# A four-stage decoder step on one core: seven products over two token chunks, in three groups per stage

## The chip, the core and the metric

The kernel runs on one core of one Trainium2 chip. The metric is the device time of one execution, in microseconds; for a kernel the median of several executions is given. The profile is that of one execution, taken by the hardware profiler. Its engines are PE (TensorE: matmuls, and PEld, its weight loads), DVE (VectorE), ACT (ScalarE), POOL (GpSimd) and SP (SyncE, which here only issues transfers). PE, DVE and ACT carry out their instructions in the order of the source (`in_order` ties each to the one before it); the order of SP's and POOL's instructions is left to the scheduler of the program.

## The reference

One inference step of a small decoder, all in float32: 1024 prompt tokens and 8 decode tokens, width 2048. The tokens are cut into two chunks: chunk 0 has 512 prompt tokens, chunk 1 has the other 512 and the 8 decode tokens (520). There are four large stages, each a product of the activations (tokens x 2048) with a weight matrix:

```python
z = x @ w_in                                   # ai: 2048 -> 2 x 2048 (u and gate)
d, state = multiscale_pool(u, prefix, pos)     # trailing windows 2, 4, 8, 16 on four channel groups
y = (group_linear(d) * scale * silu(gate)) @ w_out          # ao: 2048 -> 2048
h = layer_norm(ALPHA * x + y)
k, v = rope(h @ w_k), h @ w_v                  # bi, with the next line: 2048 -> 512 + 2 x 2048
q, gate = rope(h @ w_q), h @ w_gate
o = attention(q, k, v, window=128, sinks)      # 32 heads of 64, 4 key heads
y = (o * silu(gate)) @ w_out                   # bo: 2048 -> 2048
out = layer_norm(ALPHA * h + y)
```

So ai has 32 output tiles of 128 channels, ao 16, bi 36 and bo 16. In each stage the contraction runs over 16 blocks of 128 channels.

## The kernel before

**A product in three matmuls.** Each float32 operand is split into a high and a low part (`float32r`): ACT casts the high part (L423 for weights, L686 for activations), DVE subtracts it to get the low part (L438, L695). A block product is then high x high + high x low + low x high, three matmuls that add up in one PSUM bank (L586 to L588). A weight entry is 128 x 1024, eight blocks of 128 x 128.

**Seven products instead of eight.** The stages work by the scheme of Strassen and Winograd: two output tiles, the even and the odd contraction blocks, and the two halves of one token chunk (256 or 260 columns) form a 2 x 2 block product, done with seven half-size products, numbered 0 to 6, instead of eight. The price is sums of weight blocks (DVE, L254 and L307, stored to memory by POOL and loaded again for chunk 1) and sums of activations (`t_ops`, L741 to L744, stored as tx, tg, th and to). `seven` (L510) runs the seven products of a pair of output tiles; each is 24 matmuls. The sums that the scheme needs of results are made as banks are emptied: L527 seeds a bank with a negated result, L533 and L536 save results, L542 and L559 copy out, L547 and L552 subtract.

**Which stages run how.** `PHASES` (L50) lists the work: ai, ao, bi and bo, each for chunk 0 and then for chunk 1. Two of the nine phases, named in `PLAIN` (L57), do not use seven products: channel group 0 of ai on chunk 0, and all of bi on chunk 0. There `unit` (L600) makes one output tile with 48 matmuls of 512 columns (L614 to L616).

**Order.** All of PE's work is written out in sequence; between products `end` (L460) lets in what is due: events at a step (`at`, `product`), a step of a side task (layer norm, sums of activations or weights), and loads and splits of the next phase's activations (`x_tick`). Weights are loaded, cast and split some entries ahead (`ahead`, L185). All of these live in 53 slots of SBUF, each 128 x 1040 float32, handed out by `Mem`. The last phase ends with three tile pairs in an order of their own (`TAIL`, L68), the last half of the layer norm, and its stores.

Of the kernel before, what the change touches and what calls it, by code (L numbers as in the profile page):

```python
# [16 lines left out]
P = 128  # L17
# [20 lines left out]

NP7 = 7


# [3 lines left out]
K_ID, K_MP, K_J, K_RC = 0, 128, 256, 384  # L47
N_CST = 384 + 4 * NST
# [5 lines left out]
PHASE_OF = {"x": "ai", "g": "ao", "h": "bi", "o": "bo"}  # L54
INPUT_OF = {k: x for x, k in PHASE_OF.items()}

PLAIN = (PHASES[0], PHASES[5])  # L57
STRASSEN = [(k, c) for k, c, part in PHASES if (k, c, part) not in PLAIN]
ORDER7 = (0, 2, 1, 5, 3, 4, 6)

LOCKED = (("ao", 0), ("ao", 1), ("bi", 1), ("bo", 0), ("bo", 1))
ORDERL = (0, 5, 2, 1, 3, 4, 6)
ENGINES = (mybir.EngineType.PE, mybir.EngineType.DVE, mybir.EngineType.Activation)
NSLOT = 53
KEEP0 = 1

SPLIT = 5, 6, 7
TAIL = (  # L68
    (5, 0), (5, 2), (5, 1), (6, 0), (5, 3), (5, 4), (6, 2), (6, 1), (7, 0), (6, 3), (7, 2), (7, 1), (6, 4),
    (7, 3), (7, 4), (5, 5), (5, 6), (6, 5), (6, 6), (7, 5), (7, 6),  # L70
)
X_KEEP = 5
X_AGE = 3
SIDE_KEEP = 5

DEC_AT = (0, 1, 6, 6, 7, 8, 9, 10, 13, 13), (11, 11, 12, 12, 13, 14, 15, 16, 17, 17)
# [76 lines left out]
class Entry:  # L153


    def __init__(self, loads, make, src, after):
        self.loads, self.make, self.src, self.after = loads, make, src, after


class Kern:  # L160
    def __init__(self, ctx, tc, io):
# [19 lines left out]
        self.n = 0  # L181
        self.i = self.e = self.lastO = self.turns = self.ring = 0
        self.posts, self.events, self.side = [], {}, []
        self.fresh = False
        self.ahead = 7, 4, 3  # L185
        dr = lambda n, s: dram.tile(s, F32, tag=n, name=n)
        self.Td, self.act, self.l_sq, self.l_sh = {}, {}, {}, {}
        for c, (_, T) in enumerate(CHUNKS):
            for n, k in (("x", "ai"), ("g", "ao"), ("h", "bi"), ("o", "bo")):
                if (k, c) in STRASSEN:  # L190
                    self.Td[n, c] = dr(f"t{n}{c}", [P, 8, 4, T // 2])
            self.act["x", c] = io[f"x{c}"]
            for n in ("g", "h", "o", "p"):
                self.act[n, c] = dr(f"{n}{c}", [P, NK, T])
        self.ws = {
            n: [dr(f"s{n}{q}", [P, 4, 1024]) for q in range(np_)]
            for n, np_ in (("wia", 16), ("woa", 8), ("wkv", 2), ("wib", 16), ("wob", 8))
        }
# [10 lines left out]
    def use_four(self, wide):  # L209

        if self.four is not None:
            self.four.__exit__(None, None, None)
            self.four = None
        self.wide = wide
        if wide is None:
            return
        self.four = self.tc.tile_pool(name=self.nm("ps4"), bufs=1, space=bass.MemoryType.PSUM)
        self.pool4 = self.four.__enter__()
        if not wide:
            self.S = self.pool4.tile([P, 2, 1024], F32, name=self.nm("pS"))  # L220

    def psW(self):
        if not self.wide:
            return self.psD()
        self.turns = (self.turns + 1) % 4
        return self.pool4.tile([P, 512], F32, tag=f"W{self.turns}", name=self.nm("pD"))
# [8 lines left out]
    def split(self, hi, lo, src):  # L235
        self.nc.scalar.copy(hi, src)
        self.nc.vector.tensor_sub(lo, src, hi.bitcast(F32))


    def quads(self, name, q):  # L240
        w = self.io[name]
        u, v = w[2 * q], w[2 * q + 1]
        return u[:, :1024], u[:, 1024:], v[:, :1024], v[:, 1024:]

    def load1(self, s, k, src):
        def go():
            s[k] = self.mem.full()
            self.nc.sync.dma_start(s[k].a[:, :1024], src)

        return go  # L250

    def add1(self, s, out, a, b, dst, *free):
        def go():
            self.nc.vector.tensor_add(s[out].a[:, :1024], s[a].a[:, :1024], s[b].a[:, :1024])  # L254
            self.nc.gpsimd.dma_start(dst, s[out].a[:, :1024])
            for k in free:
                s.pop(k).free(True)

        return go

    def plain_pair(self, name, q):

        a11, a12, a21, a22 = self.quads(name, q)
        ws = self.ws[name][q]
        s = {}
        ent = lambda k, src, after: Entry([self.load1(s, k, src)], [], lambda: s[k], after)
        late = [
            self.add1(s, "c", "b", "c", ws[:, 1, :]),
            self.add1(s, "b", "a", "b", ws[:, 0, :], "b"),
            self.add1(s, "a", "a", "c", ws[:, 2, :], "c"),  # L270
            self.add1(s, "d", "a", "d", ws[:, 3, :], "a", "d"),
        ]
        return [
            ent("a", a11, []),
            ent("d", a12, []),
            ent("b", a21, []),
            ent("c", a22, [lambda: self.late.extend(late)]),
        ]

    def lone(self, src):  # L280
        s = {}
        return Entry([self.load1(s, "a", src)], [], lambda: s["a"], [lambda: s.pop("a").free()])

    def next_pair(self, name, q):
        a11, a12, _, a22 = self.quads(name, q)
        w = self.ws[name][q]
        blk = {0: a11, 1: w[:, 2, :], 2: w[:, 1, :], 3: w[:, 0, :], 4: w[:, 3, :], 5: a12, 6: a22}
        ent = {i: self.lone(blk[i]) for i in ORDER7}
        for i in (1, 2, 3, 4):
            ent[i].loads.insert(0, lambda: self.sums(name, q))  # L290
        return ent

    def first_pair(self, name, q):

        a11, a12, a21, a22 = self.quads(name, q)
        ws = self.ws[name][q]
        s = {}

        def load(k, src):
            return self.load1(s, k, src)  # L300

        def add(out, x, y, i):
            def go():
                assert self.prepped >= self.made - 2
                if out not in s:
                    s[out] = self.mem.full()
                self.nc.vector.tensor_add(s[out].a[:, :1024], s[x].a[:, :1024], s[y].a[:, :1024])  # L307
                self.nc.gpsimd.dma_start(ws[:, i, :], s[out].a[:, :1024])
# [3 lines left out]
        def free(*ks):  # L312
            return [lambda k=k: s.pop(k).free(k != "c") for k in ks]

        ent = lambda k, loads, make, after: Entry(loads, make, lambda: s[k], after)
        return {
            0: ent("a", [load("a", a11)], [], []),
            2: ent("e", [load("b", a21), load("c", a22)], [add("e", "b", "c", 1)], []),
            1: ent("a", [], [add("b", "a", "b", 0), add("a", "a", "e", 2)], free("e")),
            5: ent("d", [load("d", a12)], [], []),  # L320
            3: ent("b", [], [], free("b")),
            4: ent("d", [], [add("d", "d", "a", 3)], free("a", "d")),
# [1688 lines left out]
```

## Time and profile before

| | |
|---|---|
| median of 3 executions | 2387.29 us (2386.95 to 2390.01) |
| profiled execution, first to last instruction | 2385.9 us (its span; the profile gives no other time of it) |
| TensorE busy | 2341.5 us, 98% |
| VectorE busy | 1877.5 us, 79% |
| ScalarE busy | 1304.0 us, 55% |
| moved by DMA | 653.25 MB, 274 GB/s over the span |
| granted TensorE clock | 0.997 |

The busy times are sums over an engine's instructions with overlaps taken out. Matmuls are pipelined, so TensorE's busy time tells whether it had work, not how fast it ran; how fast is read from how many matmuls of one shape start in a stretch of time. A row of a group of instructions has the line, engine, operation, the tiles written and read with their shapes, the count, then busy time and mean duration in ns, then the idle time just before these instructions and what ended it. A row of a transfer has the size and the median time from issue to landing.

### The profile page before, as it was taken

What the parts mean: (1) busy time and instruction counts of PE and PEld (TensorE: products, weight loads), DVE (VectorE), ACT (ScalarE), POOL (GpSimd) and SP (SyncE); (2) the same over time, 40 slices, a digit from 0 to 9 for tenths busy, and PEclk for the clock granted to TensorE, in tenths of its full rate; (3) what the DMA queues carried; (4) which work ended last, traced back from release to release, by engine and by line L of the source; (5) the groups of instructions that cost most, each with busy time, mean ns of one, the idle gap of its engine ahead of it and who ended that gap; (6) DMA issues with size and microseconds to landing.
All of it is one profiled execution on the core that took longest, in us unless ns stands there. A gap on an engine that the chain in (4) does not pass through costs nothing. (4 is left out here: it accounts for less than half of the span.)

```text
span 2385.9 us, 45076 instructions
## 1 busy us (share of the span) xinstructions
PE 2341.5 (98%) x17823; PEld 2198.3 (92%) x17823; DVE 1877.5 (79%) x2315; ACT 1304.0 (55%) x2363; POOL 211.3 (9%) x373
## 2 busy tenths in 40 slices
PE   8999999999999999999999999999999999999996
PEld 6899999999999999998778888899999999999996
DVE  8797999786788768868787777777776668788877
ACT  4454446444446446653564444575666668546654
POOL 0111110000000000000011111100000000000003
PEclk9999999999999999999999999999999999999998
DMA  8667779898889888987597777589776558699883
GB/s 292 242 222 275 252 262 381 305 314 293 298 305 350 310 275 312 363 287 279 188 330 268 255 276 247 194 284 306 251 243 204 172 179 296 223 345 365 296 278 135
DMA packets 250564, 653.25 MB, mean 274 GB/s; under 512 B 25457, under 2 KB 109169, under 8 KB 250353
## 3 DMA queue, kind: packets, MB, share of 16 engines
q1 hardware_dynamic: 206032, 489.50, 61.3%
q0 software_dynamic: 44320, 160.88, 17.5%
q8 instruction: 139, 2.28, 0.4%
q14 instruction: 73, 0.59, 0.1%
HBM read 459.41 MB, written 181.36 MB: 269 GB/s over the span
## 5 line engine op out<-in xcount | busy, mean ns | idle before, releaser
L586 PE MATMUL pD<-m,m 128*128 128x260 f32 (+1 forms) x4304 | 1220.7, 284 | 6.0 <-DVE m L547 2.9
L588 PE MATMUL pD<-m,m 128*128 128x260 f32 (+1 forms) x4304 | 1212.8, 282 | 4.1 <-DVE m L438 4.1
L587 PE MATMUL pD<-m,m 128*128 128x260 f32 (+1 forms) x4304 | 1213.4, 282 | 0.0
L438 DVE TENSOR_TENSOR m<-m,m 128x1024 fp32r<-128x1024 f32 x650 | 787.5, 1222 | 102.3 <-ACT m L423 67.6
L586 PEld LDWEIGHTS pD<-m,m 128*128 128x128 f32 x4304 | 810.4, 188 | 15.3 <-issue 7.4
L588 PEld LDWEIGHTS pD<-m,m 128*128 128x128 f32 x4304 | 810.9, 188 | 5.5 <-DVE m L438 5.3
L587 PEld LDWEIGHTS pD<-m,m 128*128 128x128 f32 x4304 | 810.4, 188 | 1.6 <-issue 1.4
L423 ACT CAST m<-m 128x1024 fp32r<-128x1024 f32 x650 | 675.9, 1048 | 238.8 <-DVE m L307 56.7
L614 PE MATMUL pD<-m,m 128*128 128x512 f32 x704 | 281.4, 400 | 8.0 <-ACT m L686 8.0
L615 PE MATMUL pD<-m,m 128*128 128x512 f32 x704 | 278.1, 395 | 0.5 <-DVE m L695 0.5
L616 PE MATMUL pD<-m,m 128*128 128x512 f32 x704 | 278.0, 395 | 0.0
L614 PEld LDWEIGHTS pD<-m,m 128*128 128x128 f32 x704 | 132.9, 189 | 42.4 <-ACT m L686 8.0
L615 PEld LDWEIGHTS pD<-m,m 128*128 128x128 f32 x704 | 133.0, 189 | 30.6 <-DVE m L695 1.0
L616 PEld LDWEIGHTS pD<-m,m 128*128 128x128 f32 x704 | 132.8, 189 | 30.7
L695 DVE TENSOR_TENSOR m<-m,m 128x1024 fp32r<-128x1024 f32 (+1 forms) x114 | 139.4, 1226 | 10.6 <-ACT m L686 4.7
L559 ACT COPY m<-pD 128x260 f32<-128x260 f32 (+1 forms) x75 | 28.1, 374 | 188.7 <-PE pD L588 188.4
L686 ACT CAST m<-m 128x1024 fp32r<-128x1024 f32 (+1 forms) x114 | 119.5, 1053 | 17.6 <-PE pD L616 6.2
L254 DVE TENSOR_TENSOR m<-m,m 128x1024 f32<-128x1024 f32 x88 | 107.6, 1222 | 1.9
L1499 ACT ACTIVATE m<-m,sm 128x128 f32<-128x128 f32 x256 | 99.3, 391 | 0.0
L547 DVE TENSOR_TENSOR m<-pD,m 128x260 f32<-128x260 f32 (+1 forms) x78 | 33.1, 424 | 81.4 <-PE pD L588 81.3
L954 PE MATMUL pD<-m,m 128*128 128x260 f32 (+1 forms) x528 | 91.3, 323 | 0.0
L552 DVE TENSOR_TENSOR m<-pD,m 128x260 f32<-128x260 f32 (+1 forms) x76 | 32.2, 424 | 70.7 <-PE pD L588 70.6
(199 smaller groups left out, 2153.3 us busy)
## 6 DMA issues: line engine op xcount, KB each, us to landing
m<-in_wia SPq DMA_DIRECT2D x112, 512.0 KB, 6.9
m<-in_wib SPq DMA_DIRECT2D x112, 512.0 KB, 5.1
swia<-m POOLq DMA_DIRECT2D x64, 512.0 KB, 4.7
m<-swia SPq DMA_DIRECT2D x64, 512.0 KB, 6.6
m<-swoa SPq DMA_DIRECT2D x64, 512.0 KB, 6.8
swib<-m POOLq DMA_DIRECT2D x64, 512.0 KB, 5.0
m<-swib SPq DMA_DIRECT2D x64, 512.0 KB, 5.3
m<-swob SPq DMA_DIRECT2D x64, 512.0 KB, 6.5
```

Source lines behind the costliest of these rows:

```text
L254: self.nc.vector.tensor_add(s[out].a[:, :1024], s[a].a[:, :1024], s[b].a[:, :1024])
L423: self.nc.scalar.copy(hi.r[:, :1024], self.stream[self.cast].src().a[:, :1024])
L438: self.nc.vector.tensor_sub(lo.r[:, :1024], s.src().a[:, :1024], hi.a[:, :1024])
L586: nc.tensor.matmul(ps[:, :TH], wh[:, s], h, start=new and k == 0, stop=False, skip_group_check=on)
L587: nc.tensor.matmul(ps[:, :TH], wh[:, s], l, start=False, stop=False, skip_group_check=on)
L588: nc.tensor.matmul(ps[:, :TH], wl[:, s], h, start=False, stop=k == 7, skip_group_check=on)
L614: nc.tensor.matmul(ps[:], wh[:, s], h, start=par == 0 and k == 0, stop=False)
L615: nc.tensor.matmul(ps[:], wh[:, s], l, start=False, stop=False)
L616: nc.tensor.matmul(ps[:], wl[:, s], h, start=False, stop=par == 1 and k == 7)
L686: self.nc.scalar.copy(h.r[:, :n], s.a[:, :n])
L695: self.nc.vector.tensor_sub(l.r[:, :n], s.a[:, :n], h.a[:, :n])
L1499: nc.scalar.activation(x["s3"][:, i, :], x["s3"][:, i, :], AF.Exp, bias=nm[:, i : i + 1], scale=0.125, accum_out=rs[:, i : i + 1],)
```

## The change

The kernel's schedule is written anew. All four stages now use seven products for every pair of output tiles, and the 2 x 2 blocks are cut differently: the two columns of blocks are the two token chunks themselves (512 and 520 columns) and no longer the two halves of one chunk. There is then one phase per stage and no plain one. A pair is two output tiles half a stage apart (`positions`); there are 50 pairs: 16 in ai, 8 in ao, 18 in bi, 8 in bo.

A weight entry, once split, serves 512 or 520 columns: products 0 and 5 as 24 matmuls of 512, the other five as 2 x 24 of 260. So there are 350 weight entries of pairs plus 16 of the group products, where before every chunk had its own.

Each stage runs in three groups, one after the other over all its pairs: A (products 0 and 5, which need only chunk 0 and give chunk 0's first tile), C (1, 3 and 6, which give chunk 0's second tile), and B (2 and 4, which give chunk 1's two tiles). What one group leaves for a later one goes through memory: product 0, negated, is stored after A and loaded to seed the banks of C (`seed`), and products 1 and 3 are saved as a pair after C and loaded in B (`recall`). The sums of weight blocks are made in C and two of them stored for B.

The layer norm of chunk 0 runs during group B, that of chunk 1 during group A of the next stage; attention of chunk 0 runs during A and C of bi, that of chunk 1 during B and the start of bo. Work beside the products is placed in two ways: at a fixed step (`on`, a step being 24 matmuls of 260 or 12 of 512 columns), or softly (`soft`), between an earliest step and a due step, when an estimate of DVE's and ACT's load (`meter`, `calm`) allows it.

```diff
-PHASES = (
-    ("ai", 0, (0, 1)), ("ai", 0, (1, 4)), ("ai", 1, (0, 4)), ("ao", 0, None), ("ao", 1, None), ("bi", 0, None),
-    ("bi", 1, None), ("bo", 0, None), ("bo", 1, None),
-)
...
-PLAIN = (PHASES[0], PHASES[5])
...
-ORDER7 = (0, 2, 1, 5, 3, 4, 6)
...
+GROUPS = (("A", (0, 5)), ("C", (1, 3, 6)), ("B", (2, 4)))
+JS = {"ai": (0, 1, 2, 3), "ao": (0, 1, 2, 3), "bi": (0, 1, 2, 3), "bo": (0, 2, 1, 3)}
...
+HV = slice(0, THM), slice(THM, TMAX)
+FULL = slice(0, TP)
...
+L_LOAD, L_CAST, L_LOW = 11, 6, 4
+SLACK = 1.5
+X_LOAD, X_CAST, X_LOW, X_FAR, X_SPARE = 9, 4, 3, 22, 8
...
+    def gentle(self):
+
+        self.meter()
+        while True:
+            best = None
+            for z in self.tasks:
+                if z[2] <= self.i and (best is None or z[:2] < best[:2]) and (z[0] <= self.i or self.calm(z[3])):
+                    best = z
...
+    def sums(self, t, ph, p):
...
+        for n, k, src in ((15, "b", a21), (14, "c", a22), (13, "a", a11), (12, "d", a12)):
+            self.on(t - n, load(k, src), 6)
+        def chain(n):
+            (add("e", "b", "c", ws[:, 0, :]), s3, add("a", "a", "e"), s4)[n]()
+            if n < 3:
+                self.soft("v", self.i, t - 8 + n, lambda: chain(n + 1))
+
+        self.soft("v", t - 11, t - 9, lambda: chain(0))
...
+    def run_unit(self, u):
...
+        wh, wl = (s.r for s in self.w_get(u))
+        last = self.lastu[ph, idx] is u
+        hs = u.hs[:1] if u.grp == "A" else u.hs
+        for n, cs in enumerate(hs):
+            w = cs.stop - cs.start
+            key = ph, pos, cs.start
+            if idx in (0, 2):
+                self.bank[key] = self.psD()
+            new = idx in (0, 2)
+            ps = self.bank[key]
+            for n2 in range(8):
+                j, kk = JS[ph][n2 // 2], n2 % 2
+                k = 2 * j + kk
+                hx, lx = self.x_get((ph, idx, j))
+                h, l = (a.rv(2, TMAX)[:, kk, cs] for a in (hx, lx))
+                s = slice(k * P, (k + 1) * P)
+                on = not new
+                nc.tensor.matmul(ps[:, :w], wh[:, s], h, start=new and n2 == 0, stop=False, skip_group_check=on)
+                nc.tensor.matmul(ps[:, :w], wh[:, s], l, start=False, stop=False, skip_group_check=on)
+                nc.tensor.matmul(ps[:, :w], wl[:, s], h, start=False, stop=n2 == 7, skip_group_check=on)
...
+    def post(self, u, cs):
...
+        if idx == 0:
+            s = self.mem.half()
+            nc.gpsimd.memset(s.a[:, w:], 0.0)
+            nc.scalar.mul(s.a[:, :w], ps[:, :w], -1.0)
+            nc.gpsimd.dma_start(self.n0[ph][:, pos, :], s.a)
+            s.free(True)
+        elif idx in (1, 3):
...
+            if ph in RES:
+                nc.vector.scalar_tensor_tensor(
+                    z, z, ALPHA, ps[:, :w], op0=ALU.mult, op1=ALU.add if i else ALU.subtract
+                )
+            else:
+                nc.scalar.copy(z, ps[:, :w])
+            if idx == 3 and fin:
+                nc.gpsimd.dma_start(self.bb[ph][:, pos], s.v(2, TMAX))
...
+        elif idx in (5, 6):
...
+            self.evac(ph, pos)(self.dest(ph, pos, m, 0)(cs), ps[:, : cs.stop - cs.start])
...
+    def seed(self, u):
...
+        def load():
+            s["n"] = self.mem.half()
+            self.nc.sync.dma_start(s["n"].a, self.n0[ph][:, pos, :])
+
+        def put(h):
+            cs = HV[h]
+            ps = self.bank[ph, pos, cs.start] = self.psD()
+            self.nc.scalar.copy(ps[:, :THM], s["n"].a[:, cs])
...
+        self.on(t - 9, load, 5)
...
+        self.on(t - 2, lambda: put(0), 0)
+        self.on(t - 1, lambda: put(1), 0)
...
+    def tail_part(self, q, pos, m, cs):
...
+        if q == 3 and final:
+            square(j)
+            self.product(0 if j else 1, lambda: self.tail_sums(h, (j,), j == 0, j == 1), 1)
+            return
```

In both stages with a residual (ao, bo) the residual is added as banks of products 1 and 3 are emptied, on DVE. The attention's own arithmetic, the pooling, the group products, the layer norms' formulas and the outputs are as before.

More of the change, by code (lines that the diff above doesn't have):

```diff
@@ L252, in add1 @@
[L252 to L308, printed above, removed]
-            return go
[L312 to L322, printed above, removed]
-            6: ent("c", [], [], free("c")),
-        }
@@ L446, in flush, with end @@
+    def end(self):
         todo, self.posts = self.posts, []
@@ L468, in end @@
+        self.gentle()
         self.i += 1
         self.x_tick()
[L470 to L482 removed]
@@ new lines, in tail_stats @@
+    def tail_stats(self, h):
+        nc = self.nc
+        if not self.L:
+            two = [s.a[:, i * TMAX : (i + 1) * TMAX] for s in (self.mem.full(), self.mem.full()) for i in range(2)]
+            self.L.update(zip("mrqv", two))
+        mb, vb = self.R[h.start]
+        m, r, qq, v = (self.L[k][:, h] for k in "mrqv")
+        nc.scalar.copy(m, mb[:, :THM])
+        nc.vector.tensor_mul(qq, m, m)
+        nc.vector.scalar_tensor_tensor(v, vb[:, :THM], EPS, qq, op0=ALU.add, op1=ALU.subtract)
+        self.rstd(v, r, qq)
```

1981 lines of the change are left out of this document (970 added, 1011 removed).

## The prediction

> **What bounds the kernel now.** I read four views in this order: the busy totals, the waits of TensorE, the windows of clean stretches, and the timeline at both ends.
>
> ```profile
> span 2385.9 us, 45076 instructions
> PE 2341.5 (98%) x17823; PEld 2198.3 (92%) x17823; DVE 1877.5 (79%) x2315; ACT 1304.0 (55%) x2363; POOL 211.3 (9%) x373
> ```
> ```profile
> PE pD L614 <- ACT m L686: 8.0, 1, 8.0
> PE pD L588 <- DVE m L438: 4.1, 4, 1.3
> PE pS L1463 <- DVE m L1435: 3.4, 3, 2.2
> PE pD L586 <- DVE m L547: 2.9, 4, 1.1
> PE pD L574 <- ACT m L559: 1.6, 2, 1.4
> PE pD L1216 <- DVE m L1206: 1.6, 1, 1.6
> PE pD L586 <- ACT pD L527: 1.5, 3, 0.8
> PE pD L586 <- ACT m L423: 1.0, 1, 1.0
> PE pD L586 <- ACT m L859: 0.6, 1, 0.6
> PE pD L615 <- DVE m L695: 0.5, 1, 0.5
> ```
>
> TensorE is busy 98% of the span, and everything that it waited for is the ten rows above: 8.0 us before the first product, and 17.2 us in all the rest together. VectorE at 79% is the next engine. So the time is the sum of the matmuls' issue intervals, and a change is priced by the matmuls it removes and by the waits it makes. A matmul's own duration (282 ns) is no price, since matmuls overlap; the interval is read from stretches that hold one shape only:
>
> ```profile
> 30.00:80.00 50.00, 50.00 (x217) 40.51 (x217) 41.47 (x51) 18.40 (x26) 5.54 (x12) 1.00 0.73 252
> 850.00:900.00 50.00, 50.00 (x426) 50.00 (x425) 33.27 (x33) 24.62 (x34) 1.07 (x2) 1.00 0.78 256
> 1000.00:1050.00 50.00, 50.00 (x419) 50.00 (x419) 30.11 (x29) 21.86 (x32) 1.59 (x3) 1.00 0.91 332
> ```
>
> The columns are the stretch, then busy time and count of PE, PEld, DVE, ACT and POOL, the granted clock, the DMA share and GB/s. 30 to 80 is the plain stage (512 columns): 50/217 = 230.4 ns each. 850 to 900 is seven products on chunk 0 (256 columns): 117.4 ns. 1000 to 1050 is the same on chunk 1 (260 columns): 119.3 ns. The clock is at 1.00 throughout.
>
> **Term 1, the products.** Both programs' matmuls can be counted in their instruction order. The shapes before, as the profile has them (each row is one of three lines of equal count; 32 more of each width, into pO, belong to it):
>
> ```profile
> L586 PE MATMUL pD<-m,m 128*128 128x260 f32 x2768 | 788.4, 285 | 5.0 <-DVE m L547 2.9 <-ACT pD L527 1.5 <-ACT m L859 0.6
> L586 PE MATMUL pD<-m,m 128*128 128x256 f32 x1536 | 432.4, 281 | 1.0 <-ACT m L423 1.0
> L614 PE MATMUL pD<-m,m 128*128 128x512 f32 x704 | 281.4, 400 | 8.0 <-ACT m L686 8.0
> ```
>
> Before: 3 x 2800 = 8400 of 260 columns, 3 x 1568 = 4704 of 256, 3 x 704 = 2112 of 512. That is 1002.1 + 552.2 + 486.6 = 2040.9 us. After: 50 pairs of output tiles, each with products 0 and 5 as 24 matmuls of 512 columns and the other five as 2 x 24 of 260: 2400 and 12000. That is 553.0 + 1431.6 = 1984.6 us. The difference is **-56.3 us**. It comes from the two stages that ran plain (group 0 of the first projection on chunk 0, and the third stage on chunk 0), whose eighth product goes. The group matmuls, the attention, the transposes and the mean sums have the same counts in both programs; nine throwaway matmuls of 260 columns go (-1.1 us).
>
> [...]
>
> **Term 2, the other engines.** Every high/low weight pair now serves a whole chunk row instead of a half, so the preparation falls from 650 pairs to 366.
>
> ```profile
> L438 DVE TENSOR_TENSOR m<-m,m 128x1024 fp32r<-128x1024 f32 x650 | 787.5, 1222 | 102.3 <-ACT m L423 67.6 <-DMA swob<-m 7.3 <-PE pD L616 7.0
> L423 ACT CAST m<-m 128x1024 fp32r<-128x1024 f32 x650 | 675.9, 1048 | 238.8 <-DVE m L307 56.7 <-DVE m L438 28.2 <-PE pO L954 24.8
> L254 DVE TENSOR_TENSOR m<-m,m 128x1024 f32<-128x1024 f32 x88 | 107.6, 1222 | 1.9
> L547 DVE TENSOR_TENSOR m<-pD,m 128x260 f32<-128x260 f32 x50 | 21.3, 426 | 53.5 <-PE pD L588 53.5
> L527 ACT ACTIVATE pD<-pD 128x260 f32<-128x260 f32 x49 | 18.1, 370 | 43.0 <-PE pD L588 42.7
> ```
>
> That is 284 x 1.222 = 347 us off VectorE and 284 x 1.048 = 298 us off ScalarE. Both were beside the matmuls, so they are worth nothing directly; they are the cover for what is added. Added on ScalarE: 100 seeds of a bank (370 ns each, 37 us). Added on POOL and SP: 50 stores and 50 loads of the negated first product (260 KB), 50 and 50 of the saved pair (520 KB). The densest group is C (products 1, 3, 6): a pair has six steps of 24 matmuls, 17.2 us, and needs of VectorE four adds and three low parts (8.6 us) and up to four evacuations of 0.43 us, of ScalarE three casts, two seeds and six evacuations (about 6 us). VectorE is at 60%, ScalarE at 35%: cost nothing, hidden under those 17.2 us. If the cover went, a pair would cost the uncovered part, 50 times.
>
> Bounds for what the trace of before cannot show, the new waits of TensorE: at the lower end the 17.2 us disappear too, as VectorE has room everywhere (-17); at the upper end every group C stalls as in the slower rival below. In the order of instructions every operand of a product is made at least one step before it, and every load stands three steps (8.3 to 8.6 us) ahead of the cast or add that reads it:
>
> ```profile
> m<-in_wia SPq DMA_DIRECT2D x112, 512.0 KB, 6.9
> m<-in_woa SPq DMA_DIRECT2D x48, 512.0 KB, 6.7
> m<-to SPq DMA_DIRECT2D x8, 520.0 KB, 10.0
> ```
>
> Weights land 6.7 to 6.9 us after issue (median), 1.5 us inside the lead; the sums of the activations (10.0) land outside it. Where a load is late, the cast waits on ScalarE, and behind it the evacuations and seeds, and then TensorE. SP issues in order, so bursts matter. Counting bytes by step, the program asks 32.2 MB in the first 24 steps (66.9 us), 19.0 MB in the 45.8 us around the start of the third stage, and 12.7 MB in the 23.2 us ahead of the last stage's group C.
>
> ```profile
> DMA  8667779898889888987597777589776558699883
> GB/s 292 242 222 275 252 262 381 305 314 293 298 305 350 310 275 312 363 287 279 188 330 268 255 276 247 194 284 306 251 243 204 172 179 296 223 345 365 296 278 135
> DMA packets 250564, 653.25 MB, mean 274 GB/s; under 512 B 25457, under 2 KB 109169, under 8 KB 250353
> ```
>
> The best slice moved 381 GB/s. At that rate the bursts take 84.5, 49.9 and 33.3 us: 17.6, 4.1 and 10.1 us too long. A bank has two steps (5.6 us) in the first group before it is written again, and the loads have their 1.5 us; beyond that I expect some 10 us at the start, 5 us ahead of the last stage, and 10 us of scattered waits as in the rows of before. So I take 25 us of waits instead of 17.2: **+8 us**, nearer the lower end, since the total falls (553 MB by the program against 653) and both helping engines get lighter.
>
> [...]
>
> **Term 3, the ends.** The start is the same chain (a weight, four activation blocks, cast, low part): 0.
>
> ```profile
> 2361.13 0.28 PE L588 MATMUL pD<-m,m 128*128 128x260 f32 x1
> 2362.97 3.33 PE L1216 MATMUL pD<-m,cst 128*128 128x260 f32 x14 [1.57 <-DVE m L1206]
> 2366.60 0.35 ACT L1227 COPY m<-pD 128x260 f32<-128x260 f32 x1
> 2375.53 7.03 ACT L1253 ACTIVATE m<-m,prm 128x260 f32<-128x260 f32 x14 [1.33 <-DVE m L1243]
> ```
>
> The last product starts at 2361.13, the last statistics are copied at 2366.60, the span ends at 2385.9. Between, three evacuations, adds and squares stood; the change leaves one evacuation (0.43), one square (0.41) and two sums, with 0.6 us of start: copy about 2.5 us after the last product instead of 5.4. What follows (six normalisations on VectorE, two on POOL, sixteen activations, the stores) has the same count: **-2.9 us**. If VectorE is late by then (its last steps are full), it costs that lateness, at most some 4 us.
>
> **Sum.** 2385.9 - 56.3 - 1.1 + 8 - 2.9 = 2333.6 us of span. The runs' median, 2387.29, is 1.4 us above this span; so **2335 us**.
>
> **Rivals.**
>
> *The bursts are paid in full.* All three excesses reach TensorE without slack, 32 us, on top of the old 17.2: 2385.9 - 60.3 + 32 + 1.4 = 2359 (2352 to 2382 with more bursts of the kind). For it: strict order on SP and ScalarE. Against: loads are eleven steps ahead of the product. [...]
>
> *Group C stalls at every pair (slower).* The adds of a weight block wait for its load on VectorE or, through them, the casts on ScalarE; the evacuation queued behind them is late, and the next product into the same bank, only one step (2.9 us) away, waits. Fifty pairs: it decides from 60.3 / 50 = 1.2 us each. That needs landings of about 12.7 us (three steps and one add are 9.8, plus the 2.9 of a step that the evacuation can be late). The chip has shown 10.0 us, for eight loads. At 2 us per pair the time is 2385.9 - 60.3 + 100 + 1.4 = 2427. Against: median landings of 5 to 7 us and a smaller total.
>
> *No waits at all.* VectorE never late, the 17.2 us go: 2385.9 - 60.3 - 17.2 + 1.4 = 2310. For it: 347 us off VectorE, which ends half of the waits. Against: the bursts.
>
> That the change does not do what it says is excluded: the counts are those of the built program.
>
> **How the numbers follow.** Forecast (2318 to 2351) 0.62; bursts in full (2352 to 2382) 0.17; group C at 2 us or more (above 2392) 0.13; no waits (below 2318) 0.05; between 2382 and 2392, within 0.2%, which is about what a measurement tells from no change, 0.03. The range from 2316 to 2378 leaves out the slower case and the ends. Faster: 0.62 + 0.17 + 0.05 = 0.84; same 0.03; slower 0.13.
>
> **What would show it.** Right: matmuls of 512 columns at 217 per 50 us and of 260 at 419; 366 low parts; waits of TensorE of some 25 us beside the first 8, the longest in the first 90 us and around the last stage's group C; DMA near 560 MB. Wrong: repeated waits of the products of group C on bank seeds or evacuations; loads landing above 10 us; a tail above 22 us after the last product.

## The result

The changed kernel takes 2352.84 us (median; 2351.58 to 2355.16) against 2387.12 us before (2386.37 to 2390.01): a ratio of 0.9854, 95% interval 0.984 to 0.9868. That is 34 us faster where 52 were forecast; it lies inside the range, 18 us above the predicted 2335. The profiled execution has a span of 2351.4 us.

First rows from the profile of the changed kernel: busy time, share and instructions of each engine, the total of its transfers, and the group of the low parts (count, busy time, mean ns of one).

```profile
PE 2297.0 (98%) x16998; PEld 2134.2 (91%) x16998; DVE 1550.3 (66%) x1884; ACT 1029.2 (44%) x2071; POOL 208.1 (9%) x424
DMA packets 194481, 555.63 MB, mean 236 GB/s; under 512 B 31088, under 2 KB 36080, under 8 KB 194288
L392 DVE TENSOR_TENSOR m<-m,m 128x1024 fp32r<-128x1024 f32 x366 | 444.7, 1219 | 181.4 <-ACT m L384 167.1
```

TensorE is still the bound, VectorE fell from 79% to 66%, the low parts from 650 to 366, and 556 MB are moved instead of 653. Two clean stretches of the same kernel (columns as in the prediction), one of 512 columns and one of 260:

```profile
50.00:100.00 50.00, 50.00 (x217) 40.46 (x216) 27.92 (x37) 16.96 (x23) 8.21 (x21) 1.00 1.02 357
250.00:300.00 50.00, 50.00 (x419) 50.00 (x418) 33.77 (x35) 18.09 (x37) 5.38 (x12) 1.00 0.68 224
```

The intervals are those of before, 217 and 419 matmuls per 50 us. The waits of TensorE (total, times, longest); three more rows hold 2.0 us:

```profile
PE pD L588 <- DVE m L641: 10.9, 5, 6.1
PE pS L1429 <- DVE m L1492: 10.6, 4, 4.6
PE pD L588 <- ACT m L515: 7.9, 1, 7.9
PE pS L1483 <- ACT m L1478: 1.7, 1, 1.7
...
```

Beside the first 7.9 us they add up to 25.2 us, the 25 that the prediction took. But at the start, where it saw 10 us, there are only 0.9 us, and around the last stage's group C there are none. 20.5 us stand in two other places: attention scores that wait for the copies emptying the score bank (L1492, 10.6 us), and product 4 in the last group, which waits until VectorE has emptied product 2's result out of the bank they share (L641, 9.9 of its 10.9 us).

What the prediction had no term for is in the clock. Short stretches of the changed kernel, with TensorE's busy time and count, granted clock, DMA share and GB/s:

```profile
1182.80:1186.20 3.40, 1.11 (x5) 1.00 1.02 412
1186.20:1189.60 3.40, 1.12 (x6) 0.50 1.03 418
1189.60:1193.00 3.40, 3.40 (x16) 0.50 0.45 181
...
1964.40:1967.80 3.40, 3.33 (x52) 1.00 0.22 83
1967.80:1971.20 3.40, 3.40 (x26) 0.50 0.05 11
...
2319.40:2322.80 3.40, 1.24 (x11) 1.00 0.56 210
2322.80:2326.20 3.40, 3.40 (x16) 0.50 0.21 83
```

While products run, four stretches are at half clock, from 1186.2, 1967.8, 2285.3 and 2322.8 us on, 6.83, 6.83, 6.83 and 3.41 us long in the trace's record of the clock (the third is not shown). Three follow waits (4.6, 6.1 and 2.2 us); the second follows decode's 64 small score products, with no wait at all. In the kernel before, the record shows none from 14.6 us, where it begins, until the products are over. In this execution the stretches begin on one grid of 3.41 us (the later three start 781.66, 1099.09 and 1136.64 us after the first: 229, 322 and 333 steps), whose steps are called slots below. In the stretches, matmuls of 512 columns start 427 ns apart instead of 232, those of 260 columns some 217 instead of 120 (medians). TensorE was at work in 4.5, 6.8, 4.5 and 3.4 us of them; with half of that taken as lost, the estimate is 9.6 us (the distances between starts, taken as in the account below, give 9.3).

The account, from the trace's start times: each matmul's distance to the next one, minus the median distance of the matmuls of its source line and shape, is excess, and the medians alone are the nominal time.

| us | before | after | difference | forecast |
|---|---|---|---|---|
| nominal intervals | 2313.0 | 2256.6 | -56.5 | -57.4 |
| excess that is waits | 17.2 | 25.2 | +8.0 | +8 |
| excess at half clock (the estimate) | 0 | 9.6 | +9.6 | none |
| other excess | 28.2 | 31.3 | +3.1 | none |
| first matmul's start, and from the last one to the end | 27.5 | 28.8 | +1.3 | -2.9 |
| span | 2385.9 | 2351.4 | -34.5 | -52.3 |

### The profile page after: what moved, and what is told of

Read it like the earlier page. It is cut to its first block, busy times and chain, and to the rows that moved or that the text cites. A ratio compares the mean times of both kernels' runs of the same rounds, so it can differ in the third digit from the quotient of the medians.

```text
span 2351.4 us, 41872 instructions
## 1 busy us (share of the span) xinstructions
PE 2297.0 (98%) x16998; PEld 2134.2 (91%) x16998; DVE 1550.3 (66%) x1884; ACT 1029.2 (44%) x2071; POOL 208.1 (9%) x424
## 5 line engine op out<-in xcount | busy, mean ns | idle before, releaser
L588 PE MATMUL pD<-m,m 128*128 128x260 f32 (+1 forms) x4800 | 1463.1, 305 | 19.0 <-DVE m L641 10.9
L589 PE MATMUL pD<-m,m 128*128 128x260 f32 (+1 forms) x4800 | 1448.4, 302 | 0.9 <-DVE m L521 0.9
L590 PE MATMUL pD<-m,m 128*128 128x260 f32 (+1 forms) x4800 | 1448.0, 302 | 0.0
L392 DVE TENSOR_TENSOR m<-m,m 128x1024 fp32r<-128x1024 f32 x366 | 444.7, 1219 | 181.4 <-ACT m L384 167.1
L384 ACT CAST m<-m 128x1024 fp32r<-128x1024 f32 x366 | 380.2, 1045 | 77.6 <-PE pD L589 15.2
L428 DVE TENSOR_TENSOR m<-m,m 128x1024 f32<-128x1024 f32 x200 | 243.8, 1219 | 20.2 <-PE pD L589 6.5
L625 ACT COPY m<-pD 128x260 f32<-128x260 f32 x136 | 51.1, 376 | 225.8 <-PE pD L590 225.6
L521 DVE TENSOR_TENSOR m<-m,m 128x1040 fp32r<-128x1040 f32 x112 | 135.2, 1235 | 16.9 <-ACT m L515 16.6
L515 ACT CAST m<-m 128x1040 fp32r<-128x1040 f32 x112 | 114.7, 1059 | 37.4 <-DMA m<-h 17.8
L1492 DVE TENSOR_TENSOR m<-pS,cst 128x1024 f32<-128x1024 f32 x32 | 39.1, 1222 | 93.8 <-ACT m L1491 93.7
L1465 ACT ACTIVATE m<-m,sm 128x128 f32<-128x128 f32 x256 | 99.2, 391 | 0.0
L641 DVE TENSOR_TENSOR m<-m,pD 128x260 f32<-128x260 f32 x100 | 42.2, 422 | 75.3 <-PE pD L590 75.2
L1030 PE MATMUL pD<-m,m 128*128 128x260 f32 (+1 forms) x576 | 91.5, 319 | 0.0
L1478 ACT ACTIVATE m<-m,sm 128x128 f32<-128x128 f32 x256 | 81.8, 393 | 7.2 <-DVE sm L1473 7.1
```

Source lines behind the costliest of these rows:

```text
L384: self.nc.scalar.copy(e["hi"].r[:, :1024], e["raw"].a[:, :1024])
L392: self.nc.vector.tensor_sub(o.r[:, :1024], s.a[:, :1024], e["hi"].a[:, :1024])
L428: self.nc.vector.tensor_add(s[o].a[:, :1024], s[a].a[:, :1024], s[b].a[:, :1024])
L515: self.nc.scalar.copy(h.r[:, : 2 * TMAX], s.a[:, : 2 * TMAX])
L521: self.nc.vector.tensor_sub(o.r[:, : 2 * TMAX], s.a[:, : 2 * TMAX], h.a[:, : 2 * TMAX])
L588: nc.tensor.matmul(ps[:, :w], wh[:, s], h, start=new and n2 == 0, stop=False, skip_group_check=on)
```

## Experiments

The changed kernel's 2352.8 us is what each is compared with.

**e1. Decode's score products in two steps.** 64 matmuls of 64x8 take 4.6 us in the changed kernel's profile, the last 2.0 of them at half clock; the kernel before had issued them 32 at a time.

```diff
-        def s0():
-            open_()
-            for pr in range(2):
+        def s0(pr):
+            if pr == 0:
+                open_()
+            if True:
...
-            (0, s0, 2), (1, s1, 3),
+            (0, lambda: s0(0), 2), (1, lambda: s0(1), 2), (1, s1, 3),
```

> The 64 small score products of decode (64x8 each), which the changed kernel issues in one go, are issued 32 at a time in two successive steps, as the kernel before did. TensorE waits for nothing at that place in the changed kernel, yet its granted clock is 0.50 for the 6.83 us that follow. Clock theory: the clock is halved after any slot of about 3.41 us in which the array did little, whether it idled or ran tiny products; 32 of them fill 2.3 us of such a slot and do not trip it. The stretch of 0.50 near 1968 us is gone, and the time falls by 3.4 us, to about 2349.4. Rival (only a wait of TensorE, or chance, lowers the clock): the stretch stays or the time stays at 2352.8.

Measured: 2354.14 us (2353.45 to 2356.68), no gain. Stretches of its profile:

```profile
1807.40:1810.80 3.40, 1.53 (x15) 1.00 0.35 136
1810.80:1814.20 3.40, 3.40 (x16) 0.50 0.00 0
1967.40:1970.80 3.40, 3.33 (x39) 1.00 0.10 37
```

The stretch behind decode is gone, as the clock theory said. But the old score waits of 1.9 and 2.3 us near 1809 and 1947 us, which no half clock had followed in the changed kernel, were now each followed by 3.41 us at half clock, an estimated 1.7 us lost twice. A slot of the grid had caught all or nearly all of the wait (1.9 us idle of 3.4 in the first row) instead of two slots sharing it (1.1 and 0.8 us, 0.9 and 1.4 us in the changed kernel, at a clock of 1.00 throughout). So in these two profiles the clock goes by the grid, and the time is not a sum of such repairs. (That 32 products are safe was too simple as well: in e6 below they fell whole into one slot, and half clock followed. In the kernel before, 32 of them from 1804.3 to 1806.2 us also lay in one slot of its grid, and it did not.)

**e4 and e9. Waits made on purpose, idle and filled.** Ahead of seven products of the first projection's third group:

```diff
+            k = pos // 2
+            if (ph, idx, n, pos % 2) == ("ai", 2, 0, 0) and 2 <= pos <= 14:
+                for _ in range((2, 4, 6, 8, 10, 12, 14)[k - 1]):
+                    nc.vector.memset(ps[:, :w], 0.0)
```

> Seven waits of TensorE of growing length are made on purpose, 23 us apart, in a stretch that has none (the third group of the first projection): ahead of a product its bank is filled with zeros 2, 4, 6, 8, 10, 12 and 14 times on VectorE (some 0.35 us each), so TensorE stands for about 0.7 to 5 us plus what VectorE is behind by, some 25 us together. Clock theory: a wait shorter than about 2 us costs its length; a longer one that empties most of one slot of 3.41 us costs 1.7 us more (3.41 us at half clock), one that empties most of two costs 3.4 us more. The stretches at half clock start on one grid of 3.41 us that runs through the whole program, so of two waits of 2 to 4 us one may trip it and the other not. Sum: about 25 us of waits and some 8 us of clock. Waits alone: the clock stays 1.00 through the seven, and the time rises by the waits only.

For e9 there follows, in the same place:

```diff
+                junk, (hx, lx) = self.psW(), self.x_get((ph, idx, JS[ph][0]))
+                for _ in range((20, 40, 56, 46, 46, 72, 96)[k - 1]):
+                    nc.tensor.matmul(junk[:, :w], wh[:, :P], hx.rv(2, TMAX)[:, 0, cs], start=True, stop=True)
```

> The seven waits made on purpose, as before (they came out as 2.6, 5.1, 7.2, 5.9, 5.9, 9.2 and 12.2 us), but TensorE fills each with throwaway matmuls of 260 columns into a spare bank: 20, 40, 56, 46, 46, 72 and 96 of them, at 119.3 ns 44.9 us of the 48.1. Clock theory (the clock follows what the array did in the slot before): no stretch at half clock in the seven, and the time is that of the changed kernel plus the waits alone, 2352.8 + 48 = 2401, where unfilled waits gave 2413.9. Rival (the clock falls for another reason that the zeros on VectorE bring with them): the stretches stay, and the time stays at 2412 to 2416.

The waits came out longer than planned: 2.5, 4.9, 7.0, 5.7, 5.7, 9.1 and 12.0 us idle, 46.9 in all (48.1 as lengthened distances between starts, the measure of the expectation). Idle, the kernel took 2413.85 us (61 more), filled 2400.1 (47 more, forecast 48). Two windows, the first with two of the waits, the second with one and the end of another; idle first:

```profile
560.00:600.00 40.00, 28.04 (x208) 0.84 0.40 119
...
680.00:720.00 40.00, 29.03 (x210) 0.80 0.35 107
```

and filled:

```profile
560.00:600.00 40.00, 39.75 (x329) 1.00 0.40 120
...
680.00:720.00 40.00, 39.58 (x331) 1.00 0.41 127
```

Useless matmuls in place of the same waits made the kernel 13.8 us faster, with the same zeros on VectorE, and kept the granted clock at 1.00 over the 260 us from 525 us on, where it was 0.89 with the waits idle. So in these two runs the halving follows what TensorE did before. How little idle time was enough, e1 shows: 1.9 us, when they fell into one slot.

**e2. The copies that empty the score bank, one step earlier.**

```diff
-        self.on(at + 7, keep, 3)
+        self.on(at + (7 if c and t in (5, 6, 7) else 6), keep, 3)
```

> The copies that empty the score bank (one on ScalarE, one on VectorE) are placed one step earlier, directly behind the transposes that they read, in 29 of 32 attention tiles (three keep their place, where no buffer is free). Nothing else changes. Clock theory: the waits of the scores on these copies (10.6 us in four) fall under 2 us, and with the 4.7 us wait near 1184 us goes the stretch at half clock behind it, 3.4 us: the time falls by about 12 us, to 2341, of which TensorE's waits show 9 and the clock 3.4. Waits alone: 9 us, to 2344. Rival (these waits only stand in for a DMA that is late anyway, since VectorE stood behind a transfer for 6.5 us at 1177): the waits move to other products and the time stays within 3 us of 2352.8.

Measured: 2351.18 us (2350.42 to 2353.41), 1.7 less, within the spread of both; the rival's case. The waits at 1184, 1810 and 1878 us went. But right behind the transposes the copies make VectorE stand still, and what is queued behind them comes late. VectorE of this kernel, then the waits of its TensorE:

```profile
1322.27 1.22 DVE L1492 TENSOR_TENSOR m<-pS,cst 128x1024 f32<-128x1024 f32 x1 [3.98 <-ACT m L1491]
...
1324.54 2.38 DVE L521 TENSOR_TENSOR m<-m,m 128x1040 fp32r<-128x1040 f32 x2
```
```profile
PE pD L589 <- DVE m L521: 4.0, 6, 2.6
PE pS L1429 <- DVE m L1492: 2.8, 1, 2.8
PE pS L1429 <- DVE m L1400: 2.3, 7, 0.4
```

The 2.6 us on an activation's low part (L521) at 1323 is new, and half clock followed it: from 1327.4 us on the matmuls of 260 columns start 0.22 us apart, ahead of the wait 0.12. The wait near 1184 had another root as well, seen in the changed kernel's VectorE and TensorE, and in its transfers between 1160 and 1190 us:

```profile
1183.67 2.36 DVE L1293 TENSOR_TENSOR m<-m,m 128x1024 f32<-128x1024 f32 x2 [6.50 <-DMA m<-m]
...
1187.21 1.22 DVE L1492 TENSOR_TENSOR m<-pS,cst 128x1024 f32<-128x1024 f32 x1
...
1188.48 3.79 PE L1429 MATMUL pS<-m,m 64*128 64x256 f32 x16 [4.57 <-DVE m L1492]
```
```profile
m<-m SPq DMA_DIRECT2D x4, 128.0 KB, 11.0
```

The rotation of a query tile (L1293) waited 6.5 us for its swapped copy. The four such copies took 11.0 us to land (median) while the DMA engines were full (a share of 1.00 from 1171.0 to 1183.6 us); the copies of another tile stood behind it in VectorE's order, and the scores behind those. This is a burst that was paid, in the layer norm and attention of the third stage, where the prediction had counted none.

**e3. The last group with less work on VectorE.**

```diff
-            if p < 8:
+            if p < 8 and (c or name):
                 t = self.pair_view(pre[p], T)
                 if c == 0:
                     nc.vector.tensor_sub(t, t, b2(mu))
                 nc.vector.tensor_mul(t, t, b2(rr))
```

> Leaves out the subtraction of the mean and the product with the inverse deviation in the last layer norm of chunk 0 (16 VectorE operations of 1.22 us, 19.6 us in the last 33 steps), so that the first output is not normalised. Theory: in the last group VectorE is as full as TensorE (75.7 of 90 us busy from 2240 to 2330), and the waits on late evacuations there (11.0 us), the half-clock stretches behind them (5.1 us) and the lateness at the end (2.4 us) all come from that. They go: the time falls by 16 to 18 us, to about 2336. Waits alone: 11 us, to 2342. Rival (the last group waits for loads, on the one queue in order): the same waits stay and the time falls by less than 3 us.

Measured: 2338.98 us (2338.11 to 2344.48), 13.9 faster. What is left of its waits on the two banks:

```profile
PE pS L1429 <- DVE m L1492: 9.2, 4, 3.2
...
PE pD L588 <- DVE m L641: 1.0, 1, 1.0
```

The waits on L641 fell from 10.9 to 1.0 us, and the granted clock is 1.00 from 2225 to 2320 us, where it was 0.96 in the changed kernel. So in the last group it is VectorE's queue that is late, not a load. In the changed kernel six operations of it (two of a pair's sums, a shift, a low part, two of the normalisation) stood ahead of the subtraction that frees the bank:

```profile
2280.05 1.23 DVE L1170 TENSOR_TENSOR m<-m,m 128x1040 f32<-128x1040 f32 x1
...
2285.89 1.23 DVE L901 TENSOR_TENSOR m<-m,m 128x1024 f32<-128x1024 f32 x1
2287.03 0.42 DVE L641 TENSOR_TENSOR m<-m,pD 128x260 f32<-128x260 f32 x1
```

**e5 and e6. ScalarE empties the bank; and that with attention edits.**

```diff
-            if m:
+            if m and ph == "bo":
+                nc.scalar.copy(out, ps[:, :w])
+                nc.vector.tensor_sub(out, z[:, 1, cs], out)
+            elif m:
                 nc.vector.tensor_sub(out, z[:, 1, cs], ps[:, :w])
...
-        self.at(0, square)
         if q != 3:
-            self.at(1, add)
+            self.at(1, square)
+            self.at(2, add)
             return
+        self.at(0, square)
```

e6 adds e1's edit and places the copies early for three tiles: `6 if (c, t) in ((0, 1), (1, 2), (1, 4)) else 7`. In both, one pair's addition comes behind the last sums that should hold it, so the second half of chunk 1 is normalised with wrong statistics; the number and length of the instructions do not depend on that order.

> In the last stage product 2's bank is emptied by a copy on ScalarE (some 0.38 us), and VectorE subtracts afterwards in the buffer (0.42 us as before), so that product 4, which goes on in the same bank, waits for ScalarE and no longer for VectorE. The squares of the last pairs and the additions of them stand one step later. Theory (VectorE late by its own full queue, and the bank tied to it): the waits on those evacuations (11.0 us in five, 8.5 of them in two) fall under 3 us, the stretches at half clock near 2285 and 2323 us, which cost 4.0 us of busy time, go with them: the time falls by about 12 us, to 2341, near that of the run without the normalisation (2339.0). Rival (ScalarE runs in order too, behind squares and activations that wait for VectorE): the waits stay under another name, and the time falls by less than 4 us.

> The ScalarE evacuation of the run beside it, decode's score products in two steps, and three attention tiles alone (the second of chunk 0, and two of chunk 1) with their copies one step earlier, chosen where the scores waited. Theory: 12 us from the last group; waits of 4.7, 2.0 and 2.0 us at 1184, 1810 and 1878 us go, with 2.3 us of busy time at half clock behind the first; decode's stretch gives 3.4: together some 26 us, 2327. Rival (the waits move on to the next late operation, as they did when all tiles were moved, and stretches at half clock fall elsewhere by chance): some 14 us, 2339.

Measured: 2352.01 us (2347.39 to 2353.31) and 2351.29 (2348.97 to 2353.23). e5 gains 0.8 us, the rival's case; e6 misses both cases. Waits in e5's profile:

```profile
PE pS L1433 <- DVE m L1496: 11.5, 4, 5.4
...
PE pD L588 <- ACT m L641: 4.0, 3, 2.5
PE pD L1235 <- ACT m L1196: 1.9, 1, 1.9
```

The last group did improve (excess after 2250 us 9.6 instead of 14.7 us), with part of the waits under ScalarE's name. But ahead of it, where the program is that of the changed kernel, the excess was 56.0 instead of 51.4 us: the wait near 1184 was 5.4 us, and one more slot at half clock stands at 1152. In e6 two of the three tiles were not those that the scores waited for (the waits at 1810 and 1878 stayed), and with its copies out of the way the score at 1184 waited 2.9 us for its own late query. Decode's products, 32 at a time, were followed by half clock here:

```profile
1968.60:1972.00 3.40, 3.33 (x39) 1.00 0.23 83
1972.00:1975.40 3.40, 3.40 (x10) 0.50 0.49 154
```

They ran from 1969.4 to 1971.3, inside one slot; in e1 the slot's border (1967.8) cut 0.25 us off them.

**e10. The changed kernel once more.** No edit.

> The changed kernel itself, once more, beside the run that follows. In three kernels that are the same up to some place, waits of 2.0 and 2.4 us near 1810 and 1948 us were followed by half clock in some and not in others, by where the grid of 3.41 us fell. If the grid's phase alone decides, the same waits appear here within 0.5 us of their length, those above 4.5 us are again followed by half clock, and those of 2 us may or may not be; the time lies within 4 us of 2352.8. If the stretches belong to the kernel's places, the same four appear.

Measured: 2355.09 us (2351.1 to 2356.31). The waits were the same within 0.4 us, and the four stretches came again within 2.5 us of their places, but a fifth followed 1.75 us of idle time ahead of a tile's transposes:

```profile
1147.20:1150.60 3.40, 1.65 (x9) 1.00 0.34 140
1150.60:1154.00 3.40, 3.40 (x10) 0.50 0.84 227
```

So in the two profiles of this kernel half clock followed the longest waits both times (6.1 us, and 4.6 and 4.2 near 1184), those of some 2 us by the phase of the grid; this may be part of the spread of 4 or 5 us between executions, of which only one is profiled.

**e7. Weights loaded two steps later.**

```diff
-L_LOAD, L_CAST, L_LOW = 11, 6, 4
+L_LOAD, L_CAST, L_LOW = 9, 6, 4
...
-        for n, k, src in ((15, "b", a21), (14, "c", a22), (13, "a", a11), (12, "d", a12)):
+        for n, k, src in ((13, "b", a21), (12, "c", a22), (11, "a", a11), (11, "d", a12)):
```

> Every load of a weight block stands two steps (5.7 us) later in the order: 9 instead of 11 steps ahead of its product, the four blocks of a sum 13, 12, 11 and 11 instead of 15 to 12. Their lead over the cast or addition falls from three steps to one, 2.9 us, against a median landing of 5.4 us. Theory of the prediction's slower rival: what kept the waits out of group C, and the bursts from TensorE, was that lead; with it cut, ScalarE and VectorE stand for 2.5 us and more at each pair, and TensorE waits in all stages, 1 to 2 us at each of 50 pairs: 2400 to 2450. Rival (the transfers are far from mattering; casts and additions run late enough anyway): within 5 us of 2352.8.

Measured: 2372.89 us, 20 slower; between both. New waits beside the old ones:

```profile
PE pD L588 <- ACT pD L677: 5.1, 2, 4.2
PE pD L588 <- DVE m L621: 2.7, 2, 2.2
PE pD L588 <- ACT m L612: 2.0, 1, 2.0
```

They are five; the longest stand at 72 us and from 2081 to 2094 us: at the start and at the head of the last stage's group C, where the prediction had placed its bursts. With the full lead they cost next to nothing; with a lead of one step they cost 9.8 us of waits, and by the mean granted clock, 0.988 instead of 0.991, half clock takes an estimated 7 us more than in the changed kernel. Repeated waits at every pair, the slower rival, do not come even then.

**e8. The low parts given back to VectorE.**

```diff
+                self.lows = getattr(self, "lows", 0) + 1
+                if self.lows * 284 // 366 > (self.lows - 1) * 284 // 366:
+                    self.nc.vector.tensor_sub(o.r[:, :1024], s.a[:, :1024], e["hi"].a[:, :1024])
```

> 284 of the 366 low parts are computed twice, 347 us of VectorE, as much as the change took off. The prediction's claim (that relief lay beside the matmuls and was worth nothing directly): the time rises by 0 to 10 us. Theory after the runs before this one (in the last group VectorE is as full as TensorE, and each late copy or evacuation is paid in waits and clock): 12 or 13 more low parts in the last group add 15 us there, and 5 to 15 us come in the attention and elsewhere: 2372 to 2385.

Measured: 2411.12 us (2408.48 to 2413.76), 58 slower, and slower than the kernel before (ratio 1.0099, interval 1.0079 to 1.012). Both expectations were too low. The head of its profile and its two longest lists of waits:

```profile
PE 2311.2 (96%) x16998; PEld 2142.5 (89%) x16998; DVE 1889.6 (79%) x2168; ACT 1031.4 (43%) x2073; POOL 208.1 (9%) x424
...
PE pS L1432 <- DVE m L1495: 20.2, 9, 9.8
PE pD L591 <- DVE m L644: 20.0, 8, 10.2
```

VectorE at 79%, as before the change, hides behind the old order of work and not behind the new one.

**e11 and e12. Edits put together.** e11 has e5's evacuation with the addition ahead of the sums (rank 0), the last group's weights loaded, cast and split two to four steps earlier, e1's edit, the copies of tiles 1 and 3 of chunk 1 early, and all eight tiles of chunk 0 in group A one step later (`a + 21`). e12 leaves out the earlier weights and shifts the third tile alone:

```diff
-                self.attend(0, 2 * n + i, a + 20 + 16 * n + 8 * i)
+                self.attend(0, 2 * n + i, a + 20 + 16 * n + 8 * i + (n == 1 and i == 0))
...
-        self.on(at + 7, keep, 3)
+        self.on(at + (6 if (c, t) in ((0, 2), (1, 1), (1, 3)) else 7), keep, 3)
```

In e11, with all eight tiles shifted, chunk 0's attention is no longer what the reference computes, nor is the first output; its instructions are the same in number.

> Five edits: in the last stage product 2's bank is emptied by ScalarE, with the squares and additions one step later but ahead of the last sums; the low parts of the last group's weights are made two to four steps earlier; decode's score products in two steps; the attention tiles of chunk 0 start one step later, so that the transfer their score waits for near 1184 us has landed; the copies of two tiles of chunk 1 (the second and fourth of its second head half) one step earlier, since the scores at 1810 and 1878 us waited for them. Theory: some 8 us in the last group (the same evacuation brought the excess after 2250 us from 14.7 to 9.6 us), 5 us at 1184 with its clock, 4 us at 1810 and 1878, 3.4 us behind decode: 2332. Rival (waits and half-clock slots turn up elsewhere as fast as they are removed): 2345 to 2352.

> Of the five edits, the earlier low parts are left out, and instead of all eight attention tiles of the first group only the third of chunk 0 is placed one step later, its copies keeping their step (the one whose score waited near 1184 us for a transfer). All outputs are computed. Theory: the waits at 1184, 1810 and 1878 us and the stretches at half clock behind the first and behind decode go, as they did in the run with five edits (excess up to the last group 13 us less), and the evacuation by ScalarE brings the 3 to 5 us that it showed twice in the last group: 2335 to 2338. Rival (the evacuation brings nothing when the work reaches the last group in another phase): 2340 to 2343. If the shift of all eight tiles was needed, the waits near 1184 stay: 2345 or more.

Measured: 2341.03 us (2339.52 to 2342.52) and 2344.33 (2343.68 to 2346.74), the second with a ratio to the kernel before of 0.9824, 0.981 to 0.9837. e11 lies between its two cases; e12 is 1.3 us above its rival's. e12 is thus faster than both kernels, by 8.5 us than the changed one (0.9854, 0.984 to 0.9868). In it the waits near 1184, 1810 and 1878 us and decode's stretch are gone (excess up to 2250 us 39.2 instead of 51.4 us), though new half-clock slots stand at 1151.8 and 1940.3 us. But the last group gave nothing (14.9 instead of 14.7):

```profile
PE pD L588 <- ACT m L641: 7.8, 3, 3.6
PE pD L1235 <- DVE m L1200: 2.5, 1, 2.5
PE pS L1433 <- DVE m L1496: 2.3, 1, 2.3
```

There ScalarE is late in VectorE's place: the copy at 2273.8 us was itself held 4.6 us, until an addition on VectorE (L1174) was done, the other two stood in order behind activations that wait for VectorE, and the later additions reach into the last sums (L1235). The full worth of that group, the 14 us of e3, needs less work on VectorE there; no run found a way to it that leaves the output whole.

## Why the prediction was right or wrong

- *The bound, and Term 1:* right. The intervals did not change, and the nominal time fell by 56.5 us of the 57.4 forecast for matmuls and throwaways.
- *Term 2, "worth nothing directly; they are the cover for what is added":* right as it stands, and more than it said: the cover is needed. Giving VectorE as much work back (79%, e8) costs 58 us, so without that relief the change would, as far as that run tells, have been slower.
- *Term 2, "I take 25 us of waits instead of 17.2: +8 us":* this is the step that failed. The sum was met to the microsecond, by chance: of the 15 us placed at the start and ahead of the last group C at most 0.9 came (the lead covers the rest; e7), and 20.5 us came from the bank of scores and the bank of the last group, which were counted only as "scattered". In the first 67 us the transfers moved 26 of the 32 MB counted there, at 392 GB/s, and TensorE waited 0.9 us: the rest was not needed yet. The step also priced a wait at its own length. Three waits, and decode's products now issued together, were each followed by half clock: an estimated 9.6 us with no term (e4, e9).
- *"VectorE is at 60%, ScalarE at 35%: cost nothing":* true for group C, where that tally was made, but not for the last stage's group B, which was not tallied: there VectorE is busy for 71 of 95 us (2225 to 2320), in bunches, and product 4 needs the bank one step after product 2 (e3).
- *Term 3, "-2.9 us":* -0.4 when counted as there, from the last product to the end (24.7 us before, 24.3 after); the +1.3 of the account count the end from the last matmul of any kind. The last statistics are copied 4.5 us after the last product, not 2.5, since ScalarE is late by then:

```profile
2327.85 1.50 ACT L887 ACTIVATE m<-m,prm 128x512 f32<-128x512 f32 x2
2329.26 0.40 ACT L1193 ACTIVATE m<-m 128x260 f32<-128x260 f32 x1
2329.57 2.07 ACT L1261 ACTIVATE m<-m,prm 128x260 f32<-128x260 f32 x4
2331.55 0.35 ACT L1243 COPY m<-pD 128x260 f32<-128x260 f32 x1
```

  The last square (2329.26) stood behind activations of the two normalisations still under way (L887 is chunk 0's), and the copy behind four more (L1261); the lateness that was allowed for VectorE came from ScalarE, and the end behind the copy took 19.8 us against 19.3.
- *The rivals:* the time lies above the band given to the forecast itself (2318 to 2351), at the lower edge of "bursts in full" (2352 to 2382), yet of the three bursts named there only the first cost anything, at most 0.9 us. One burst that nobody named was paid, 4.6 us at 1184. "Group C stalls" stayed out by a good margin: even with 5.7 us of the lead gone there were five waits and not fifty. Of the other signs of being wrong, two came: a tail of 24.3 us, above 22, and landings of 11.0 us, above 10 (in the kernel before the longest median of a load was already 10.4, for the eight of swkv, not 10.0).

What stays open: the 3.1 us of other excess, small differences over the stretch with the attention; and whether the waits that e12 still has can go without new ones.

## What to carry to other kernels

When TensorE is the bound, price a wait twice: by its length, and by what the granted clock does behind it. In the profiles of this case 1.9 us of idle time in one slot of 3.41 us (e1) were followed by 3.41 us at half clock, and 64 matmuls of 64x8 acted as such a wait. Tally the helping engines group by group and look for the result that must leave a shared bank within one step: VectorE, at 66% on average, was late where its work was bunched (71 of 95 us). Expect repairs of single waits to return less than their length, and test the repair of a place by taking work off the late engine before moving work about.

## What the runs showed of the hardware that was not expected

- The granted clock went to 0.50 after slots of 3.41 us with about half or more of them idle on TensorE. In the profiles of the two kernels, each of the five slots at full clock with 2.16 us or more of idle time was followed by half clock, and none with 1.57 us or less, small products aside, so not the 1.4 us of the wait at 1946 us in the changed kernel, shared by two slots. In between lie 1.87 us in e1 and 1.75 us in e10, both followed by half clock. Small products acted much like idle time: 64 of 64x8 in a row (4.6 us) were followed by half clock in the changed kernel, and again in e10; 32 (1.96 us) were in e6, where they fell whole into one slot, but not in the kernel before, where the first 32 also did, nor in e1.
- Transfers reached 424 GB/s over 3.4 us in both kernels (from 663.0 us before, from 2067.2 us after); the 381 of the best slice before is a mean over 59.6 us. With the DMA engines full (share 1.00, around 1177 us), copies of 128 KB within the chip took 11.0 us to land.
